# Hybrid trunk layer on one core: large loads on ScalarE's DMA queue, Gram matrices of the delta rule issued ahead of the substitution

## The chip, the cores and the metric

The kernel runs on one NeuronCore of a Trainium2 chip. TensorE (PE) multiplies matrices, VectorE (DVE), ScalarE (ACT) and GpSimd (POOL) work on tiles, and each of SyncE (SP), ScalarE and GpSimd can issue transfers. The metric is the time of one execution on the device, in microseconds, lower is better; several runs are made and their median is compared.

## The reference

One layer: RMSNorm of x with 16 learned meta tokens put in front (2048 + 16 tokens of 1024 channels), one projection to 8208 columns, two groups of heads on them, an output projection of 2048 channels added to x, and a final RMSNorm. Cut to what matters:

```python
h = rmsnorm(x, norm_g)
p = h @ w_in                                  # q k v | z | a b | sc_b sc_c sc_h sc_z
qkv = silu(causal_dwconv(qkv, dn_conv_w))     # width 4
q, k = l2norm(q) * 128 ** -0.5, l2norm(k)     # 8 heads x 128
g = -exp(A_log) * softplus(a + dt_bias); beta = sigmoid(b)
# gated delta rule in chunks, with decay = exp(g_i - g_j):
a_low = strict_lower(beta_i * (k k^T) * decay)
u, w = solve(I + a_low, [v * beta, k * beta * exp(g)])
for each chunk:                               # the scan over chunks
    v_new = u - w S
    o = (q exp(g)) S + ((q k^T) * decay) v_new
    S = S * exp(g_last) + (k exp(g_last - g))^T v_new
o_dn = rmsnorm(o, dn_out_g) * silu(z)
o_sc = sc_b * causal_dwconv(sc_c * sc_h, sc_conv_w) * silu(sc_z)
return rmsnorm(x + concat(o_dn, o_sc) @ w_out, final_g)
```

## The kernel before

All is float32; a large matmul is done as three float32r matmuls on parts hi and lo (hi x hi, lo x hi, hi x lo), so a weight tile is needed as `wh` and `wl`.

The first phase runs over two halves of 1024 tokens (the first with the meta tokens). A half has 64 jobs: 8 slots (one for each head and one eighth of the short convolution) of 8 column tiles of 128 (k, q, v, z and the four of the short convolution). A job (`run_group`, L745) runs three groups of tokens, each 24 matmuls into one of the PSUM tiles `mm`, which ScalarE or VectorE evacuates (`raw`, `acc`, `sc_c`, `zs`). `load_w` (L716) fetches a job's 512 KB of `w_in` into one of the two tiles `wr`; `split_w` (L722) makes `wh` on ScalarE and `wl` on VectorE in two halves, and gives the load of the job after the next right behind the second.

Beside the jobs run streams, Python generators that give work in small steps between a job's matmuls. `delta_front` (L971) does, for one half of one head at a time (a "half head", 16 in all; here "head 14" counts them from 0): the decays `E`, the Gram matrices k k^T and q k^T of two chunks of 128 tokens at a time (their operands' hi and lo parts in tile `nb`), the triangular matrices `M` and `P`; then the diagonal 32 x 32 blocks of `M` go by DRAM (`nbd`) into `nb`, where 31 rows of a substitution on VectorE (`substitution`, L942: a product `prod<-nb,XT` and a sum `XT<-prod` for each) give their inverses `XT`, which go to DRAM (`xtd`). `delta_back` loads these into `W`, transposes them (`X`) and merges them by matmuls (`ta<-X,E`) into the inverses of whole chunks; `delta_scan` runs the recurrence (`rec`, `vn`, `S`, `os`), `delta_out` norms and stores the outputs.

A small model of the engines (L30 to L100), written into the program, decides when a stream gives its next step; the order on each engine's queue is fixed when the program is built. A generator can also wait on a key in `done`, or on a tile in `held` (`hold`, L590). All engines' work goes through one recorder, so every row says L118: a tile's name tells what it is.

All transfers are issued by SP, in one queue: the weight loads, the small round trips by `nbd` and `xtd`, the decays, the gates and the stores `mixd` of the outputs. The second phase multiplies `mixd` by `w_out`; `load_mix` (L1425) brings the mixed channels of a tile of 128 tokens into `wr`.

Of the kernel before, what the change touches and what calls it, by code (L numbers as in the profile page):

```python
# [29 lines left out]
class Model:  # L30
    """Time of each engine and of each tile, as work is issued; it decides the order of issue only."""
# [32 lines left out]
    def after(self, *aps, slot=None, eng=None, lag=0.0, least=0.02):  # L64
        """Time until the tiles are written, the slot is free and the engine is through but for lag."""
# [96 lines left out]
class Recorded:  # L162
    """The engines of a core, with all that they are given entered into the model."""

    def __init__(self, nc, model):
        self.tensor = _Engine(nc.tensor, "PE", model)
        self.vector = _Engine(nc.vector, "DVE", model)
        self.scalar = _Engine(nc.scalar, "ACT", model)
        self.gpsimd = _Engine(nc.gpsimd, "POOL", model)
        self.sync = _Engine(nc.sync, "DMA", model)  # L170


@with_exitstack
def hybrid_trunk(
# [41 lines left out]
    # ---- order of emission: a stream of projections, cut into pieces, and streams of dependent  # L216
    # steps that are issued between the pieces. `model` follows the engines as they are given work;
    # a step yields the time until what its successor needs is there.
# [28 lines left out]
    def when_done(fn, ap, most=100.0):  # L247
        """Issue fn once ap has been written."""
        timed.append((clk() + min(after(ap), most), fn))
# [46 lines left out]
    def newton(dst, a, y, t):  # L296
        """dst = y (1.5 - 0.5 a y^2): one Newton step for a ** -0.5 from y."""
# [19 lines left out]
    # ---- constants of the first phase  # L317
# [12 lines left out]
    # eyep[32 q + block, m, i] = (i == 8 q + m)  # L330
    eyep = vt(pp, [128, 8, 32], "eyep")
# [10 lines left out]
    def constants():  # L342
# [29 lines left out]
        nc.gpsimd.memset(eyep, 0.0)  # L372
        for q in range(4):
            for m in range(8):
                nc.gpsimd.memset(eyep[32 * q : 32 * q + 32, m, 8 * q + m : 8 * q + m + 1], 1.0)
# [13 lines left out]
    def turn(hf, xt, k0, i, col, n, g):  # L389
        """Channels 4 k0 .. 4 k0 + 3 of a token tile into h^T."""  # L390
# [18 lines left out]
    def statistics(xt, n, jk):  # L409
        """mean square + eps and its approximate power -0.5."""  # L410
# [6 lines left out]
    def rootmean(xt, n):  # L417
        """(mean square + eps) ** -0.5 by ACT and GpSimd."""
# [14 lines left out]
    def prologue0():  # L433
        """h^T = (RMSNorm(x))^T of the first half as float32r parts hi + lo, [channel, k, token]
        by group."""
# [100 lines left out]
    def normalize(i):  # L536
        """RMSNorm of token tile i of the second half, to DRAM until the first half is through."""
        xt = vt(dp, [128, NC, 128], "kd").rearrange("p c i -> p (c i)")
        nc.sync.dma_start(xt, xs[HALF + 128 * i :][:128])
        yield after(xt)  # L540
        st = statistics(xt, 128, vt(dp, [128, 1840], "gw", dt=BF16))
# [48 lines left out]
    def hold(tag="ta", keep=False):  # L590
        """Wait until no step holds tag over several yields; or hold it."""
# [7 lines left out]
    def gates(hf):  # L599
        """Token-major gate values [128, head, chunk]; on half 0 chunk 8 holds the meta tokens."""  # L600
# [21 lines left out]
        gw = vt(dp, [128, 920], "gw")  # L622
# [24 lines left out]
        # e = exp(-|a|), exp(-|b|), exp(min(b, 0))  # L647
# [11 lines left out]
        # log1p(e) = 2 atanh(s), s = e / (2 + e) <= 1 / 3  # L659
# [34 lines left out]
        nc.sync.dma_start(ged[hf, :Wd], gT[:Wd])  # L694
        G[hf] = dict(beta=beta, gcum=gcum, neg=neg, nch=nch)
# [3 lines left out]
    # ---- projections  # L699
    class Job:  # L700
        def __init__(self, hf, col, init, consume, fin=None, skip=False):
# [8 lines left out]
            self.begun = False  # L710

# [3 lines left out]

    def load_w(j):  # L716
        if j < len(jobs):
            J = jobs[j]
            J.wr = vt(wp, [128, KT, 128], "wr")
            nc.sync.dma_start(J.wr, win[:, :, J.col : J.col + 128])  # L720

    def split_w(j, eng=None):  # L722
        if j >= len(jobs):
            return
        J = jobs[j]
        J.wh = vt(wp, [128, KT, 128], "wh", dt=F32R)
# [3 lines left out]
        if eng is not None:  # L730
            eng.tensor_tensor(out=J.wl, in0=J.wr, in1=J.wh, op=ALU.subtract)
            load_w(j + 2)
# [3 lines left out]
        def half(i):  # L736
            s_ = slice(4 * i, 4 * i + 4)
            nc.vector.tensor_tensor(out=J.wl[:, s_], in0=J.wr[:, s_], in1=J.wh[:, s_], op=ALU.subtract)
            if i == 1:
                load_w(j + 2)  # L740
# [35 lines left out]
    def conv_job(hf, s, col, t, pre, emit):  # L776
        """Projection, causal width-4 convolution and SiLU of channel tile t of q | k | v."""
# [43 lines left out]
    def slot_jobs(hf, s):  # L821
# [51 lines left out]
        # short convolution of channel tile s  # L873
# [67 lines left out]
    # ---- gated delta rule  # L941
    def substitution(nb, XT, prod):  # L942
        """Rows of (I + N)^-1 of unit lower triangular 32 x 32 blocks, a block and 8 columns per
        partition; nb[j, i] = N[i, j], XT[col, i], prod[col, i] = identity on entry."""
# [9 lines left out]
    def decay(hf, row0, n, E, gc):  # L954
        """E[j, c, i] = exp(g_i - g_j) for i >= j, else 0."""
# [14 lines left out]

    def delta_front():  # L971
        """Decays, the two triangular matrices, and the inverses of the diagonal blocks."""
        for i in range(2 * NH):
# [14 lines left out]
            )  # L988
            if hf == 0:
                Em = vt(dp, [NM, 1, NM], "mE")  # L990
# [20 lines left out]
            for c2 in range(4):  # L1011
                c0 = 2 * c2
                yield after(slot=(dp, "nb"))
                kp = vt(dp, [128, 2, 2, 2, 128], "nb", dt=F32R)
# [11 lines left out]
                for c in range(2):  # L1026
# [4 lines left out]
                    mmr(o_, lhsT=l_[:, :128], rhs=h_, start=False, stop=True)  # L1031
                yield after(pm, E)
# [27 lines left out]
            # inverses of the 32 x 32 diagonal blocks: partition 32 q + 8 b + c, columns 8 q .. 8 q + 7  # L1060
# [8 lines left out]
            if hf == 0:  # L1069
                yield from meta_inputs(hd, g_, d, Em)  # L1070
            yield after(nb)
# [12 lines left out]
            nc.gpsimd.tensor_copy(prod, eyep)  # L1084
# [20 lines left out]
            half[i] = dict(M=M, P=P, cd=cd, ir=ir, cj=cj)  # L1105
            done.add(("front", i))

    def delta_back():
        """The inverses of the whole chunks, and what the scan needs by token."""
        for i in range(2 * NH):  # L1110
# [11 lines left out]
            # q exp(g); token-major k, q norms, v  # L1122
# [514 lines left out]
```

## Time and profile before

| what | value |
| --- | --- |
| median of 3 runs | 2257.49 us (2250.55 to 2260.83) |
| span of the profiled execution | 2248.0 us, 9.5 below the median and 2.6 below the fastest run |
| TensorE busy | 2175.4 us (97%) |
| VectorE, ScalarE, GpSimd busy | 1456.6, 864.9, 153.3 us |

The busy share is an average over a start in which the pipeline fills, 16 slots of projections and a second phase of matmuls alone. The span less TensorE's time is what a change of order can take away; which wait ends last is read from the waits and from the timeline at each place. A wait is named by engine, the tile whose instruction waited, and what ended it; "issue" is a wait for which the profile shows no releaser.

### The profile page before, as it was taken

What the parts mean: (1) busy time and instruction counts of PE and PEld (TensorE: products, weight loads), DVE (VectorE), ACT (ScalarE), POOL (GpSimd) and SP (SyncE); (2) the same over time, 40 slices, a digit from 0 to 9 for tenths busy, and PEclk for the clock granted to TensorE, in tenths of its full rate; (3) what the DMA queues carried; (4) which work ended last, traced back from release to release, by engine and by line L of the source; (5) the groups of instructions that cost most, each with busy time, mean ns of one, the idle gap of its engine ahead of it and who ended that gap; (6) DMA issues with size and microseconds to landing.
All of it is one profiled execution on the core that took longest, in us unless ns stands there. A gap on an engine that the chain in (4) does not pass through costs nothing.

```text
span 2248.0 us, 38710 instructions
## 1 busy us (share of the span) xinstructions
PE 2175.4 (97%) x15024; PEld 2061.8 (92%) x15024; DVE 1456.6 (65%) x4031; ACT 864.9 (38%) x2080; POOL 153.3 (7%) x312
## 2 busy tenths in 40 slices
PE   6999999999999999999999999999998799999998
PEld 6999999999999998999999999999998798888886
DVE  4676867676767767776868677676766465544322
ACT  5534434444444333443434343525352324422111
POOL 4000100000000000101000000000000000000000
PEclk9999999999999999999999999999999899999999
DMA  6444345443535677524343544253546664645321
GB/s 140 75 81 70 84 68 91 67 93 67 92 67 104 82 83 60 134 43 80 52 83 57 78 52 83 48 88 43 88 49 60 53 94 139 222 164 189 119 94 57
DMA packets 257237, 196.46 MB, mean 87 GB/s; under 512 B 62085, under 2 KB 226446, under 8 KB 257054
## 3 DMA queue, kind: packets, MB, share of 16 engines
q1 hardware_dynamic: 257054, 194.00, 47.5%
q8 instruction: 118, 1.93, 0.4%
q14 instruction: 65, 0.53, 0.1%
HBM read 157.89 MB, written 36.06 MB: 86 GB/s over the span
## 4 chain that ended last, share of the span: by engine, by line
PE 87%; DMA 6%; DVE 4%; SPq 1%; ACT 1%; issue 1%; POOL 0%; POOLq 0%; DVEq 0%; ACTq 0%
PE mm L118 74%; PE ta L118 7%; PE rec L118 4%; PE o L118 2%; SPq L118 1%; DMA nb<-nbd 1%; DMA wr<-in_w_in_dram 1%; DMA kd<-in_x_dram 1%; DVE prod L118 1%; DMA xtd<-XT 1%; DMA W<-xtd 1%; ACT junk L118 1%; DVE acc L118 1%; DVE XT L118 1%; DMA nbd<-E 0%
## 5 line engine op out<-in xcount | busy, mean ns | idle before, releaser
L118 PE MATMUL mm<-hh,wh 128*128 128x384 f32 (+3 forms) x3328 | 1043.6, 335 | 6.4 <-ACT hh L118 5.3
L118 PE MATMUL mm<-hl,wh 128*128 128x384 f32 (+3 forms) x3328 | 1015.1, 326 | 0.0
L118 PEld LDWEIGHTS mm<-hh,wh 128*128 128x128 f32 x3328 | 626.8, 189 | 21.0 <-ACT hh L118 5.9
L118 PEld LDWEIGHTS mm<-hl,wh 128*128 128x128 f32 x3328 | 627.3, 189 | 9.7
L118 PE MATMUL mm<-hh,wl 128*128 128x384 f32 (+3 forms) x3200 | 622.6, 327 | 2.8 <-DVE wl L118 2.8
L118 PEld LDWEIGHTS mm<-hh,wl 128*128 128x128 f32 x3200 | 512.6, 189 | 9.9 <-DVE wl L118 3.2
L118 DVE TENSOR_TENSOR wl<-wr,wh 128x512 fp32r<-128x512 f32 x348 | 233.8, 691 | 98.8 <-ACT wh L118 67.0
L118 DVE SCALAR_TENSOR_TENSOR acc<-raw,pcol,acc 128x384 f32<-128x384 f32 (+2 forms) x432 | 245.5, 573 | 60.5 <-ACT acc L118 55.9
L118 ACT ACTIVATE wh<-wr 128x1024 fp32r<-128x1024 f32 x178 | 187.8, 1055 | 79.3 <-PE mm L118 44.5
L118 DVE SCALAR_TENSOR_TENSOR prod<-nb,XT 128x8 f32<-128x8 f32 (+30 forms) x496 | 192.8, 389 | 39.1 <-DMA nb<-nbd 34.0
L118 DVE TENSOR_REDUCE XT<-prod 128x8 f32<-128x16 f32 (+30 forms) x496 | 147.2, 297 | 17.0
L118 ACT ACTIVATE raw<-mm 128x272 f32<-128x272 f32 (+2 forms) x144 | 65.7, 456 | 214.1 <-PE mm L118 214.1
L118 ACT ACTIVATE vn<-rec,cj 128x128 f32<-128x128 f32 x128 | 46.9, 366 | 252.0 <-PE rec L118 246.7
L118 ACT ACTIVATE sc_c<-mm 128x384 f32<-128x384 f32 (+4 forms) x99 | 45.0, 456 | 161.8 <-PE mm L118 158.0
L118 PE MATMUL mm<-oh,wh 128*128 128x512 f32 x256 | 101.9, 398 | 0.0
L118 PE MATMUL mm<-ol,wh 128*128 128x512 f32 x256 | 100.3, 392 | 0.0
L118 DVE TENSOR_TENSOR y<-mm,y 128x512 f32<-128x512 f32 x23 | 15.9, 692 | 110.7 <-PE mm L118 110.7
L118 DVE SCALAR_TENSOR_TENSOR yy<-rec,neg,vr 128x128 f32<-128x128 f32 x128 | 44.4, 347 | 62.3 <-PE rec L118 61.8
L118 ACT ACTIVATE ojk<-y 128x512 bf16<-128x512 f32 x23 | 14.5, 631 | 182.6 <-DVE y L118 127.0
L118 ACT ACTIVATE acc<-mm,pcol 128x272 f32<-128x272 f32 (+2 forms) x144 | 78.2, 543 | 0.0
L118 DVE SCALAR_TENSOR_TENSOR S<-S,egl,rec 128x128 f32<-128x128 f32 x104 | 35.8, 344 | 59.2 <-PE rec L118 58.3
L118 POOL TENSOR_TENSOR opy<-mo,nhalf 128x4 f32<-128x4 f32 x32 | 35.3, 1102 | 544.0 <-DVE mo L118 507.3
(244 smaller groups left out, 2548.8 us busy)
## 6 DMA issues: line engine op xcount, KB each, us to landing
wr<-in_w_in_dram SPq DMA_DIRECT2D x128, 512.0 KB, 9.0
wr<-mixd SPq DMA_DIRECT2D x50, 512.0 KB, 4.5
E<-gtd SPq DMA_DIRECT2D x16, 512.0 KB, 4.1
qd<-ged SPq DMA_DIRECT2D x16, 512.0 KB, 8.4
nb<-nbd SPq DMA_DIRECT2D x64, 128.0 KB, 5.3
mixd<-zs SPq DMA_DIRECT2D x32, 256.0 KB, 3.2
out_dram<-y SPq DMA_DIRECT2D x16, 512.0 KB, 2.6
mixd<-sc_y SPq DMA_DIRECT2D x32, 192.0 KB, 2.4
```

The costliest lines, as they stand in the source:

```text
L118: r = real(*args, **kw)
```

## The change

Three things are changed; comments and docstrings go too.

1. A helper `bulk` issues a transfer on ScalarE's queue. The 128 weight loads use it, and the mix loads of the first eight tiles (32). The load of job j + 2 is no longer given right behind the second half of `wl` but when the model says that this is done; `split_w` gives it if it hasn't come. The model books 0.4 us of ScalarE for it.
2. `delta_front` ends with the Gram matrices. The blocks' way by `nbd` and `nb`, the substitution and the store to `xtd` become a stream of their own, `delta_inverse`, which waits for the Gram of its half head; `delta_front` meanwhile goes on to the next. The hi and lo parts of k and q move from tile `nb` to `gw`, which is guarded by `hold` against `gates` and `normalize`.
3. The identity for the substitution (`prod`) is made by a memset and four selects on GpSimd; before it was copied from a tile `eyep`.

```diff
+        self.bulk = _Engine(nc.scalar, "DMA", model)
...
+    def bulk(out_, in_):
+        nc.bulk.dma_start(out_, in_)
+        model.free["ACT"] = max(model.free["ACT"], clk()) + ISSUE
...
     def load_w(j):
-        if j < len(jobs):
+        if j < len(jobs) and jobs[j].wr is None:
             J = jobs[j]
             J.wr = vt(wp, [128, KT, 128], "wr")
-            nc.sync.dma_start(J.wr, win[:, :, J.col : J.col + 128])
+            bulk(J.wr, win[:, :, J.col : J.col + 128])
...
         J = jobs[j]
+        load_w(j)
...
             if i == 1:
-                load_w(j + 2)
+                when_done(lambda: load_w(j + 2), J.wl)
...
+                while i and ("meta", i - 1) not in done:
+                    yield 0.3
                 Em = vt(dp, [NM, 1, NM], "mE")
...
-                yield after(slot=(dp, "nb"))
-                kp = vt(dp, [128, 2, 2, 2, 128], "nb", dt=F32R)
+                yield after(slot=(dp, "gw"))
+                yield from hold("gw", True)
+                kp = vt(dp, [128, 2, 2, 2, 128], "gw", dt=F32R)
...
+                held.discard("gw")
...
-            # inverses of the 32 x 32 diagonal blocks: partition 32 q + 8 b + c, columns 8 q .. 8 q + 7
+            fronts[i] = (M, Em)
+            half[i] = dict(M=M, P=P, cd=cd, ir=ir, cj=cj)
+            done.add(("gram", i))
+
+    def delta_inverse():
+        for i in range(2 * NH):
+            hf, hd = divmod(i, NH)
+            while ("gram", i) not in done:
+                yield 0.3
+            d, g_ = slot[i], G[hf]
+            M, Em = fronts[i]
             nb = vt(dp, [128, 32, 32], "nb")
...
-            nc.gpsimd.tensor_copy(prod, eyep)
+            nc.gpsimd.memset(prod, 1.0)
+            for q in range(4):
+                nc.gpsimd.affine_select(
+                    out=prod[32 * q : 32 * q + 32],
...
         mr = vt(wp, [128, KT, 128], "wr")
-        nc.sync.dma_start(mr, mixd[u[0], :, KT * h : KT * h + KT])
+        (bulk if u[0] < NC else nc.sync.dma_start)(mr, mixd[u[0], :, KT * h : KT * h + KT])
```

The instructions of TensorE and VectorE stay the same in number. SP's transfers fall by 160 and ScalarE's rise by 160. Three places show the order.

On SP, around the inverse of head 14 (half head 6 of the second half), before, from the load of the blocks to the load of the inverses:

```order
L118 DMA nb<-nbd 32x1024 x4
L118 DMA qd<-ged 128x1024
L118 DMA mixd<-zs 128x4x128
L118 DMA wr<-in_w_in_dram 128x8x128 x4
L118 DMA mixd<-sc_y 128x2x128
L118 DMA mixd<-sc_y 128x3x128
L118 DMA xtd<-XT 32x8x32 x4
L118 DMA mixd<-sc_y 128x3x128
L118 DMA wr<-in_w_in_dram 128x8x128
L118 DMA W<-xtd 32x8x32 x4
```

The same place after:

```order
L118 DMA nb<-nbd 32x1024 x4
L118 DMA qd<-ged 128x1024
L118 DMA mixd<-zs 128x4x128
L118 DMA mixd<-sc_y 128x2x128
L118 DMA mixd<-sc_y 128x3x128
L118 DMA xtd<-XT 32x8x32 x4
L118 DMA mixd<-sc_y 128x3x128
L118 DMA W<-xtd 32x8x32 x4
```

The five weight loads that stood between `nb` and `W` are gone from SP's queue; the small transfers keep their order.

On ScalarE, at the end of the scan of head 13, before (`vn` and `os` belong to the scan, `raw` and `acc` evacuate a projection):

```order
L118 ACTIVATE wh<-wr 128x1024
L118 ACTIVATE vn<-rec,cj 128x128 x2
L118 ACTIVATE os<-o 128x512
L118 ACTIVATE junk,mo<-os 128x128 x4
L118 ACTIVATE wh<-wr 128x1024 x2
L118 ACTIVATE raw<-mm 128x256
L118 ACTIVATE acc<-mm,pcol 128x256
```

The same place after:

```order
L118 DMA wr<-in_w_in_dram 128x8x128
L118 ACTIVATE vn<-rec,cj 128x128
L118 ACTIVATE wh<-wr 128x1024
L118 ACTIVATE vn<-rec,cj 128x128
L118 ACTIVATE os<-o 128x512
L118 ACTIVATE junk,mo<-os 128x128 x4
L118 DMA wr<-in_w_in_dram 128x8x128
L118 ACTIVATE wh<-wr 128x1024
L118 ACTIVATE raw<-mm 128x256
L118 ACTIVATE acc<-mm,pcol 128x256
L118 DMA wr<-in_w_in_dram 128x8x128
```

Weight loads now stand among ScalarE's instructions, here one ahead of `vn`, one ahead of `wh` and one behind `acc`.

On VectorE, where the Gram of head 5 begins (`cd` copies its decays, `nb<-k,nb` and `nb<-q,nb` are the low parts of k and q, `P<-ta,E` takes the result), before, behind the last row of head 4's substitution:

```order
L118 COPY cd<-E 128x8
L118 TENSOR_TENSOR sc_u<-mm,sc_c 128x384
L118 TENSOR_TENSOR vr<-ta,ir 128x512
L118 TENSOR_TENSOR sc_y<-mm,sc_y 128x256
L118 TENSOR_SCALAR sc_y<-sc_u,pcol 128x384
L118 SCALAR_TENSOR_TENSOR sc_y<-sc_u,pcol,sc_y 128x384 x2
L118 TENSOR_TENSOR wl<-wr,wh 128x512
L118 TENSOR_TENSOR nb<-k,nb 128x2x128
L118 TENSOR_TENSOR nb<-q,nb 128x2x128
L118 STREAM_TRANSPOSE X<-W 32x8x32 x3
L118 TENSOR_TENSOR sc_y<-mm,sc_y 128x384
L118 TENSOR_TENSOR P<-ta,E 128x256
```

The same after, where these rows use the tile `gw`:

```order
L118 TENSOR_TENSOR wl<-wr,wh 128x512
L118 SCALAR_TENSOR_TENSOR prod<-nb,XT 128x8x25
L118 TENSOR_REDUCE XT<-prod 128x8
L118 TENSOR_TENSOR gw<-k,gw 128x2x128
L118 TENSOR_TENSOR gw<-q,gw 128x2x128
L118 SCALAR_TENSOR_TENSOR prod<-nb,XT 128x8x26
L118 TENSOR_REDUCE XT<-prod 128x8
L118 SCALAR_TENSOR_TENSOR prod<-nb,XT 128x8x27
L118 TENSOR_REDUCE XT<-prod 128x8
L118 TENSOR_TENSOR P<-ta,E 128x256
L118 TENSOR_TENSOR E<-ta,E 128x256
```

The low parts for head 5 now stand between rows 25 and 26 of head 4's substitution; the rows `prod<-nb,XT` go on behind them.

## Rows read from the trace of the kernel before

**Rows 1.** The page: busy time, share and instructions of each engine.

```profile
PE 2175.4 (97%) x15024; PEld 2061.8 (92%) x15024; DVE 1456.6 (65%) x4031; ACT 864.9 (38%) x2080; POOL 153.3 (7%) x312
```

**Rows 2.** Windows; columns: stretch, width, PE, PEld, DVE, ACT, POOL, PEclk, DMA share, GB/s.

```profile
0.00:50.00 50.00, 30.95 (x184) 28.48 (x185) 23.89 (x39) 26.84 (x48) 26.90 (x105) 1.00 0.68 157
...
500.00:600.00 100.00, 99.95 (x758) 97.09 (x757) 70.03 (x225) 41.02 (x109) 7.32 (x15) 1.00 0.41 75
```

**Rows 3.** Waits of PE, whole run: total us, times, longest us.

```profile
PE ta L118 <- issue: 15.0, 3, 13.6
...
PE rec L118 <- DVE os L118: 10.5, 5, 6.4
...
PE rec L118 <- DVE S L118: 7.4, 3, 3.5
...
PE ta L118 <- DVE X L118: 3.8, 2, 3.2
```

**Rows 4.** Timeline of PE: start, us, what, and in brackets the idle before.

```profile
1705.95 1.12 PE L118 MATMUL rec<-ident,os 128*128 128x128 f32 x4 [6.39 <-DVE os L118]
...
1773.24 1.48 PE L118 MATMUL ta<-X,E 32*32 32x32 f32 x32 [13.61 <-issue]
```

**Rows 5.** Timeline of DVE at the ends of its waits.

```profile
802.43 0.17 DVE L118 SCALAR_TENSOR_TENSOR prod<-nb,XT 128x8 f32<-128x8 f32 x1 [3.98 <-DMA nb<-nbd]
...
1702.65 0.17 DVE L118 SCALAR_TENSOR_TENSOR prod<-nb,XT 128x8 f32<-128x8 f32 x1 [8.72 <-DMA nb<-nbd]
...
1772.71 1.37 DVE L118 STREAM_TRANSPOSE X<-W 32x256 f32<-32x256 f32 x3 [15.91 <-DMA W<-xtd]
...
1821.60 0.17 DVE L118 SCALAR_TENSOR_TENSOR prod<-nb,XT 128x8 f32<-128x8 f32 x1 [5.20 <-DMA nb<-nbd]
```

**Rows 6.** Waits of DVE, whole run: total us, times, longest us.

```profile
DVE prod L118 <- DMA nb<-nbd: 34.0, 10, 8.7
...
DVE X L118 <- DMA W<-xtd: 20.9, 3, 15.9
```

**Rows 7.** Timeline of SP, the issue of transfers, 1755 to 1775.

```profile
1756.41 0.39 SPq L118 DMA_DIRECT2D wr<-in_w_in_dram  x1
...
1759.56 4.91 SPq L118 DMA_DIRECT2D W<-xtd  x4
```

**Rows 8.** DMA issues, 400 to 700: count, KB each, median us to landing.

```profile
wr<-in_w_in_dram SPq DMA_DIRECT2D x21, 512.0 KB, 8.7
...
xtd<-XT SPq DMA_DIRECT2D x12, 32.0 KB, 4.4
...
W<-xtd SPq DMA_DIRECT2D x12, 32.0 KB, 1.9
```

**Rows 9.** DMA issues, 1660 to 1840.

```profile
wr<-in_w_in_dram SPq DMA_DIRECT2D x10, 512.0 KB, 14.0
...
xtd<-XT SPq DMA_DIRECT2D x4, 32.0 KB, 9.5
...
W<-xtd SPq DMA_DIRECT2D x4, 32.0 KB, 13.0
```

**Rows 10.** Windows around TensorE's stops (columns as in group 2).

```profile
880.00:890.00 10.00, 10.00 (x116) 9.18 (x116) 4.82 (x15) 3.23 (x6) 0.00 (x0) 0.80 0.57 27
...
1690.00:1712.00 22.00, 15.61 (x90) 15.29 (x89) 9.79 (x33) 3.20 (x11) 1.31 (x3) 0.84 0.57 75
...
1752.00:1772.00 20.00, 7.63 (x49) 7.14 (x46) 0.77 (x2) 7.68 (x22) 0.10 (x1) 0.81 0.93 84
...
1772.00:1785.00 13.00, 11.61 (x153) 10.56 (x154) 7.53 (x19) 4.97 (x11) 0.00 (x0) 0.76 0.21 33
```

**Rows 11.** The page: costliest groups of instructions, the low part of a weight tile.

```profile
L118 DVE TENSOR_TENSOR wl<-wr,wh 128x512 fp32r<-128x512 f32 x348 | 233.8, 691 | 98.8 <-ACT wh L118 67.0
```

**Rows 12.** Groups of POOL by shape: count, busy us, mean ns, idle before.

```profile
L118 POOL COPY prod<-eyep 128x256 f32<-128x256 f32 x16 | 6.6, 411 | 0.0
...
L118 POOL TENSOR_SCALAR_AFFINE_SELECT mE<-mE 16x16 f32<-16x16 f32 x8 | 3.0, 369 | 1.1 <-DVE mE L118 1.1
```

More of the change, by code (lines that the diff above doesn't have):

```diff
@@ L329, in hybrid_trunk @@
     triu = vt(pp, [128, 128], "triu")
-    eyep = vt(pp, [128, 8, 32], "eyep")
     W = vt(pp, [128, NC, 128], "W")
@@ L371, in constants @@
         nc.gpsimd.memset(X[0:64], 0.0)
[L372 to L375, printed above, removed]
         nc.scalar.activation(negA, negA, AF.Exp)
@@ L540, in normalize @@
         yield after(xt)
+        yield from hold("gw")
         st = statistics(xt, 128, vt(dp, [128, 1840], "gw", dt=BF16))
@@ L621, in gates @@
         pt = ptile(pta, "ta", [128, 512])
-        gw = vt(dp, [128, 920], "gw")
+        yield from hold("gw", True)
+        gw = vt(dp, [128, 1024], "gw")
         ab2 = gw[:, 0:288].rearrange("p (c m) -> p c m", m=32)
@@ L710, in __init__ @@
             self.begun = False
+            self.wr = None
     jobs = []
@@ L739, in half @@
             if i == 1:
-                load_w(j + 2)
+                when_done(lambda: load_w(j + 2), J.wl)
         later(lambda: half(0))
@@ L969, in hybrid_trunk @@
     half = {}
+    fronts = {}
     def delta_front():
@@ L988, in delta_front @@
             )
+            Em = None
             if hf == 0:
+                while i and ("meta", i - 1) not in done:
+                    yield 0.3
                 Em = vt(dp, [NM, 1, NM], "mE")
@@ L1012, in delta_front @@
                 c0 = 2 * c2
-                yield after(slot=(dp, "nb"))
-                kp = vt(dp, [128, 2, 2, 2, 128], "nb", dt=F32R)
+                yield after(slot=(dp, "gw"))
+                yield from hold("gw", True)
+                kp = vt(dp, [128, 2, 2, 2, 128], "gw", dt=F32R)
                 kh, kl = kp[:, 0], kp[:, 1]
@@ L1031, in delta_front @@
                     mmr(o_, lhsT=l_[:, :128], rhs=h_, start=False, stop=True)
+                held.discard("gw")
                 yield after(pm, E)
@@ L1070, in delta_front @@
                 yield from meta_inputs(hd, g_, d, Em)
+            done.add(("meta", i))
             yield after(nb)
@@ L1083, in delta_front @@
             prod = vt(dp, [128, 8, 32], "prod")
-            nc.gpsimd.tensor_copy(prod, eyep)
+            nc.gpsimd.memset(prod, 1.0)
+            for q in range(4):
+                nc.gpsimd.affine_select(
+                    out=prod[32 * q : 32 * q + 32],
+                    in_=prod[32 * q : 32 * q + 32],
+                    pattern=[[-1, 8], [1, 32]],
+                    compare_op=ALU.is_equal,
+                    fill=0.0,
+                    base=-8 * q,
+                    channel_multiplier=0,
+                )
             rows = [substitution(nb, XT, prod)]
@@ L1104, in delta_front @@
                 )
-            half[i] = dict(M=M, P=P, cd=cd, ir=ir, cj=cj)
             done.add(("front", i))
@@ L1377, in delta_out @@
             yield 0.3
+    ISSUE = 0.4
     STEP = 1.0
@@ L1493, in hybrid_trunk @@
     start(delta_front())
+    start(delta_inverse())
     start(delta_back())
```

## The prediction

> **What bounds the kernel now.** I read the engine lines first: TensorE is busy 2175.4 of 2248.0 us, VectorE 65%, ScalarE 38%, GpSimd 7% [rows 1]. So a change can only gain in TensorE's 72.6 us of idle time and in what TensorE loses at a low clock; no matmul is added or removed here. The table of windows says where that is not: 500 to 600 us has 99.95 us of work in 100 at full clock, while the first 50 us have 30.95, that is 19.0 us of idle before anything is in the buffers [rows 2]. The waits of TensorE name the rest [rows 3]: 15.0 us of `ta` behind "issue", 10.5 `rec` behind `os`, 7.4 `rec` behind `S`, 3.8 `ta` behind `X`.
>
> Each large wait is then followed one engine back. TensorE stops 6.39 us before 1705.95, and 13.61 us before 1773.24 [rows 4]. VectorE at these places stood before its own first product of the substitution (8.72 us, `nb<-nbd`, until 1702.65) and before the transposes of `W` (15.91 us, `W<-xtd`, until 1772.71). It did so too ahead of the three `S` waits, each time for `nb`: 3.98 us at 802.43 in the first, 5.20 at 1821.60 in the last [rows 5]. Over the whole run VectorE waits 34.0 us for `nb` in 10 places and 20.9 us for `W` in 3 [rows 6]. Those are loads of 128 KB. The reader is to see in SP's timeline why they are late: at 1756.41 SP issues a weight tile of 512 KB, at 1759.56 the four `W` loads, which come to use 13 us later [rows 7]. Between 400 and 700 us a `W` load lands 1.9 us after its issue and a weight tile 8.7; between 1660 and 1840 these are 13.0 and 14.0, and `xtd` 9.5 [rows 8, 9]. `W` takes as long as the weight load ahead of it: one queue serves them in their order.
>
> **What the change does to this.** Part (a): 128 weight tiles and 32 mix tiles leave SP's queue for ScalarE's. In the first pair of orders SP had five weight loads between the `nb` loads and the `W` loads of this head; now it has none. So the 13.0 us should fall towards 1.9. What goes with it: 13.6 (the long one of the "issue" waits), 6.4 of `os`, 7.4 of `S` and 3.8 of `X`, together 31.2 us.
>
> With the idle time a second cost goes. Around each of these stops the granted clock is below 1, and half clock is the 1.2 GHz level. The time lost is the window by what the mean clock lacks, by TensorE's busy share there [rows 10]: 880 to 890: 10 x 0.20 x 1.00 = 2.0; 1690 to 1712: 22 x 0.16 x 0.71 = 2.5; 1752 to 1772: 20 x 0.19 x 0.38 = 1.4; 1772 to 1785: 13 x 0.24 x 0.89 = 2.8. That is 8.7; with the shorter dips, which I didn't add up, I take 10 us. The least is 4.8, from 880 to 890 and 1772 to 1785 alone, where TensorE was busy; in the others the low clock may have fallen in the idle part. Together 41 us are to be had.
>
> Not all of it goes. Weight tiles of the last slot land in 14.0 us and not 8.7, and the DMA share was 0.93 at 84 GB/s in 1752 to 1772: the 16 engines were busy with slow transfers, and `W` on its own queue still shares them. If it got half of these 84 GB/s, its 4 x 32 KB would take 3.1 us, with the 1.9 of an undisturbed one 5; `xtd` the same, so the round trip is 10 us, against 9.5 + 13.0 = 22.5 before and 4.4 + 1.9 = 6.3 in the middle of the first half [rows 8, 9]. The order gives the round trip about 10 to 14 us of TensorE work before the transposes come (my count of the instructions between, 75 to 105 rows at the 99.95 / 758 = 0.13 us of rows 2). So it is met at the edge. I keep a quarter of the 41, 10 us; the bounds are 0 (round trip 6.3) and 41 (nothing is won, below).
>
> The Trainium skill, "DMA: Bandwidth & Descriptors", section "Issuing engines are not separate DMA queues", speaks against the change: transfers that different engines initiate run on the same 16 DMA engines, and a second initiating engine only saves the sequencer its issue time. By that sentence alone the sum would be about 0. The section "Queues, rings and completion order" of the same page gives SP and ScalarE a ring each on every engine, served in turn packet by packet; by that, `W` passes the load ahead of it. The 1.9 against 13.0 [rows 8, 9] shows only that order in one queue costs 11 us; no run of before has loads in two queues, so the first rule is kept as a rival.
>
> Part (a) has a price on ScalarE. A weight load takes 0.39 us of issue [rows 7], and ScalarE must stop at it until the second half of `wl` has been made (0.69 us of VectorE [rows 11]), because that tile's buffer is being refilled. Queued behind it are the evacuations of PSUM and the `vn` of the scan, for which TensorE waits. In the second pair of orders a load stands right ahead of `vn` and of `wh`. In the whole order 17 of the 128 stand right ahead of a `vn`, 55 ahead of an evacuation (`raw`, `sc_c`, `zs`). An evacuation has the other PSUM buffers' matmuls as cover; `vn` lies on the scan's chain, which has projections beside it. Bounds: 0, and 17 x (0.39 + 0.69) = 18. I take half of 17 x 0.39 = 6.6: 3 us. The mix loads of the second phase cost nothing: ScalarE is idle for most of that time; if not, 32 x 0.39 = 12, at the 18's side of the range.
>
> Part (b): the Gram matrices run ahead. The third pair of orders shows it: before, decay and Gram of head 5 come after the last row of head 4's substitution, now between its rows. No instruction is added, the hi and lo tile only changes its name from `nb` to `gw`, which frees `nb` sooner. TensorE is full there (the 99.95), so what becomes ready earlier waits in the queue. I cost it at 0. If its cover goes, it adds VectorE work between rows: two subtractions per pair of chunks, already counted in the 65%. From below: it could take the remaining 10 us away, as the substitution starts sooner.
>
> Part (c): `prod` by a memset and four selects on GpSimd in the place of one copy. The copy takes 0.411 and a 16x16 select 0.369 [rows 12]; with a memset counted like the copy that is 16 x 4 x 0.369 = 24 us more of GpSimd. VectorE's first copy waits for it, 1.5 us more per head. That lies behind the `nb` load, VectorE has a third of its time idle, and TensorE has projections to do: 0, with 24 as upper bound. At the start the third weight load now stands in ScalarE's queue ahead of its evacuations: 0, bounds 5 either way, a quarter of the 19.0 [rows 2].
>
> **The sum.** 2248.0 - 41 + 10 + 3 = 2220. The profiled execution is 9.5 us below the median of the three runs (2257.49; 2.6 below the fastest), so the median is 2229.5, in whole 2229. Own range: from 2211, where all of the 41 and 5 of the start are gained and nothing is paid, to 2246, where 23 of the 41 stay and 7 are paid.
>
> **Rivals.** (A) More: the round trip has its 6.3 us, the start gains its 5: 2248 - 41 - 5 + 9.5 = 2211. For it: the Gram is ahead, and `nb` comes free earlier. Against it: the slow loads of the last slot. Chance 0.12.
>
> (B) The 16 engines are the limit, not the queue: `W` and `nb` take as long beside a load as behind it. For it: share 0.93 at 84 GB/s [rows 10]. Against it: the share is 0.41 in 500 to 600 [rows 2], so most heads meet engines with room. What is left are the `S` waits, mostly away from the slow loads: 2257.5 - 7.4 + 3 = 2253. This is also what comes if the stops only move, for instance to the weight tiles: at 14.0 us each and eight jobs a slot the loads need 112 us, and with the idle gone TensorE needs little more. Chance 0.16.
>
> (C) Slower: ScalarE is held by the loads. Place: the 72 loads ahead of `vn` and the evacuations; price: 72 x (0.39 + 0.69) = 78 us if nothing covers them, since ScalarE stands at `wl` and everything that TensorE waits for is behind. It decides over the sign once (41 - 10) / 78 = 40% of it reach TensorE. At three quarters: 2226.5 + 58 = 2285; at half 2265. For it: VectorE's own stops (15.91) would now stop ScalarE too. Against it: ScalarE has 62% idle, and the order puts the load behind the `wl` by a little. Chance 0.12 of more than 0.5% slower.
>
> That the change doesn't do what it says: the orders show it does.
>
> **Chances.** 0.5% (11.3 us) is about what a measurement of this kernel can tell from no change: 2246.2 and 2268.8 are its ends. My forecast 0.60 and (A) 0.12 are faster: 0.72. (B) is the same: 0.16. (C) is slower: 0.12. The range, 2209 to 2257, holds (A) with 2 us for idle time that I didn't count, the forecast, and (B) up to the median of before; it leaves out (C).
>
> **What would show it.** Right: VectorE's 34.0 for `nb` and 20.9 for `W` fall below 20 together; `W` lands in 2 to 6 us between 1660 and 1840; TensorE's stops of 13.61 and 6.39 are gone and its clock there is 1. (B): the landing stays near 13. (C): new TensorE waits for ScalarE (`vn`, `mm` evacuations), with ScalarE idle ahead of a load for `wl`. Wrong altogether if TensorE's busy time grows without a lower clock.

## The result: slower, 2288.4 us

The changed kernel takes 2288.39 us (median of 4 runs, 2287.56 to 2289.44), the kernel before 2255.09 (4 runs beside it); the ratio is 1.0142, interval 1.0122 to 1.0162. 2229 was predicted, with a range up to 2257. The profiled execution spans 2285.6 us, 37.6 more than before.

The page's busy line, and its rows of the two hardware queues (packets, MB, share of 16 engines; q10 carries ScalarE's transfers, q1 SP's):

```profile
PE 2194.1 (96%) x15024; PEld 2071.0 (91%) x15024; DVE 1467.2 (64%) x4031; ACT 864.2 (38%) x2080; POOL 189.1 (8%) x343
...
q10 hardware_dynamic: 137728, 83.90, 30.8%
q1 hardware_dynamic: 119326, 110.10, 15.9%
```

Against [rows 1] TensorE is busy 18.7 us longer with the same 15024 instructions, and idle 91.5 us where it was 72.6. So half of the loss is waiting, and most of the other half is a lower clock: the mean granted clock is 0.984, before 0.991, which makes 2175.4 us of work 15.5 us longer. The windows show where, with the columns of [rows 2]:

```profile
0.00:50.00 50.00, 23.22 (x146) 21.10 (x147) 24.15 (x32) 22.71 (x41) 23.91 (x68) 1.00 0.65 157
500.00:600.00 100.00, 97.48 (x729) 94.15 (x727) 70.92 (x205) 38.09 (x102) 8.76 (x17) 1.00 0.39 82
205.00:225.00 20.00, 16.08 (x83) 14.01 (x82) 12.48 (x27) 7.36 (x29) 0.00 (x0) 0.78 0.74 140
268.00:284.00 16.00, 10.34 (x47) 8.45 (x46) 15.17 (x45) 4.90 (x12) 0.00 (x0) 0.69 0.33 58
1690.00:1712.00 22.00, 22.00 (x157) 22.00 (x156) 15.34 (x50) 8.97 (x22) 0.00 (x0) 1.00 0.43 31
1795.00:1815.00 20.00, 10.58 (x119) 9.57 (x120) 7.57 (x22) 2.47 (x6) 3.98 (x8) 0.54 0.43 50
```

The stretch 1690 to 1712, with the stop of 6.39 us before [rows 4, 10], is now full and at clock 1. But 205 to 225 and 268 to 284 have new dips to 0.78 and 0.69, 1795 to 1815 has 10.58 us of work at 0.54 where 1752 to 1772 was [rows 10], and 500 to 600 is no longer full. TensorE's largest waits (total, times, longest) put names to them:

```profile
PE ta L118 <- DVE vT L118: 17.3, 1, 17.3
PE rec L118 <- ACT vn L118: 10.1, 9, 2.1
PE ta L118 <- DVE X L118: 9.8, 1, 9.8
PE ta L118 <- issue: 8.6, 4, 3.9
PE ta L118 <- DVE gw L118: 5.7, 3, 2.7
```

The waits for `os` and `S` [rows 3] fell from 10.5 and 7.4 to 4.1 and 5.4. New are those for `vn` and `gw`, and 10 us more at the start (`vT`, 17.3 where it was 6.8); one wait for `X` is still 9.8 us long. VectorE's waits for transfers, as in [rows 6]:

```profile
DVE X L118 <- DMA W<-xtd: 19.6, 5, 10.8
...
DVE vT L118 <- DMA sc_u<-in_norm_g_dram: 16.5, 1, 16.5
...
DVE prod L118 <- DMA nb<-nbd: 5.0, 3, 2.6
```

`nb` fell from 34.0 to 5.0, `W` only from 20.9 to 19.6. The issues of 400 to 700, then of 1660 to 1840, against [rows 8, 9]:

```profile
wr<-in_w_in_dram ACTq DMA_DIRECT2D x21, 512.0 KB, 8.7
...
xtd<-XT SPq DMA_DIRECT2D x12, 32.0 KB, 1.6
W<-xtd SPq DMA_DIRECT2D x12, 32.0 KB, 2.4
...
wr<-in_w_in_dram ACTq DMA_DIRECT2D x11, 512.0 KB, 13.8
...
xtd<-XT SPq DMA_DIRECT2D x8, 32.0 KB, 2.2
W<-xtd SPq DMA_DIRECT2D x8, 32.0 KB, 8.5
```

The weight loads land as before, `xtd` sooner, and the `W` loads of the last slot in 8.5 us, where 2 to 6 were the sign that the forecast was right.

To place the loss I lined up the traces by the first matmul of a job (job 64 opens the second half, the last column is a place in the second phase). Times are start in the kernel before, then microseconds later than it:

| kernel | job 8 | job 24 | job 64 | job 112 | job 124 | second phase |
| --- | --- | --- | --- | --- | --- | --- |
| before, start | 135.7 | 360.8 | 939.6 | 1618.2 | 1811.8 | 2150.9 |
| changed | 6.0 | 24.9 | 39.5 | 36.9 | 29.2 | 37.9 |
| part (a) alone (e1_queue) | 6.0 | 6.3 | 29.6 | 26.6 | 24.8 | 65.7 |
| parts (b), (c) alone (e2_gram) | -0.3 | 18.3 | 44.2 | 42.9 | 36.2 | 37.7 |
| the same, Gram ahead in the second half only (e16_half2) | -0.7 | 3.2 | 44.6 | 52.7 | 52.9 | 53.7 |

The changed kernel loses 6 us at the start, 33 in the rest of the first half, wins 10 back in the second, and loses 9 at the end. A job can also start late because other work was given ahead of it (the changed kernel is 37.5 us late at job 20), so single columns are rough. The runs of the last three rows are told below.

### The profile page after: what moved, and what is told of

Read it like the earlier page. It is cut to its first block, busy times and chain, and to the rows that moved or that the text cites. A ratio compares the mean times of both kernels' runs of the same rounds, so it can differ in the third digit from the quotient of the medians.

```text
span 2285.6 us, 38685 instructions
## 1 busy us (share of the span) xinstructions
PE 2194.1 (96%) x15024; PEld 2071.0 (91%) x15024; DVE 1467.2 (64%) x4031; ACT 864.2 (38%) x2080; POOL 189.1 (8%) x343
## 4 chain that ended last, share of the span: by engine, by line
PE 85%; DMA 6%; DVE 5%; ACT 3%; issue 1%; SPq 0%; POOL 0%; ACTq 0%; POOLq 0%; DVEq 0%
PE mm L118 71%; PE ta L118 7%; PE rec L118 4%; PE o L118 2%; DMA wr<-mixd 1%; DMA kd<-in_x_dram 1%; DMA Q<-in_norm_g_dram 1%; DVE prod L118 1%; ACT junk L118 1%; DMA W<-xtd 1%; DMA qd<-in_x_dram 1%; DVE XT L118 1%; DVE acc L118 1%; DVE wl L118 1%; DMA xtd<-XT 1%
## 5 line engine op out<-in xcount | busy, mean ns | idle before, releaser
L118 ACT ACTIVATE wh<-wr 128x1024 fp32r<-128x1024 f32 x178 | 187.9, 1056 | 97.6 <-DMA wr<-mixd 53.7
L118 ACT ACTIVATE raw<-mm 128x272 f32<-128x272 f32 (+2 forms) x144 | 65.7, 456 | 225.4 <-PE mm L118 224.9
L118 POOL TENSOR_TENSOR kpy<-ssk,nhalf 128x8 f32<-128x8 f32 x16 | 28.7, 1791 | 537.5 <-DVE ssk L118 471.4
```

The source lines that it names most:

```text
L118: r = real(*args, **kw)
```

## The experiments

Each was run in 5 rounds beside the kernel before. The medians:

| run | what | median us | ratio, interval |
| --- | --- | --- | --- |
| e1_queue | part (a) alone | 2305.9 | 1.0231 (1.0208 to 1.0253) |
| e2_gram | (b) and (c) alone | 2286.0 | 1.0138 (1.0119 to 1.0158) |
| e3_first | changed, first two weight loads on SP | 2287.2 | 1.0145 (1.0123 to 1.0166) |
| e4_mix | changed, mix loads on SP | 2276.7 | 1.0097 (1.0080 to 1.0115) |
| e5_gram2 | changed, Gram ahead in the second half only | 2320.6 | 1.0295 (1.0265 to 1.0325) |
| e6_cols | changed, the last slot's jobs load the first slot's columns | 2264.5 | 1.0036 (1.0023 to 1.0049) |
| e7_late | (a)'s time of giving, SP's queue | 2261.3 | 1.0033 (1.0021 to 1.0045) |
| e9_cols_before | before, the same | 2222.4 | 0.9852 (0.9833 to 0.9871) |
| e10_swap | before, slow column tiles shared out between two slots | 2240.1 | 0.9936 (0.9923 to 0.9949) |
| e11_rest | (a) without mix and first two loads | 2286.0 | 1.0141 (1.0122 to 1.0159) |
| e12_pool | e11's weight loads issued by GpSimd | 2274.3 | 1.0090 (1.0069 to 1.0110) |
| e15_prod | (c) alone | 2251.2 | 0.9986 (0.9978 to 0.9994) |
| e16_half2 | (b), (c), ahead in the second half only | 2306.1 | 1.0220 (1.0204 to 1.0237) |
| e17_half2_swap | the same with e10's exchange | 2297.2 | 1.0177 (1.0161 to 1.0193) |
| e18_swap_prod | before, e10's exchange and (c) | 2243.9 | 0.9949 (0.9934 to 0.9964) |
| e19_delay0 | before, first half's substitutions 5 us later | 2284.1 | 1.0123 (1.0102 to 1.0143) |
| e20_delay1 | before, second half's 5 us later | 2230.1 | 0.9890 (0.9870 to 0.9910) |
| e21_both | e10 and e20 | 2225.2 | 0.9866 (0.9849 to 0.9883) |

**The two parts apart.** e1_queue is the kernel before with the `bulk` helper, `load_w` and `load_mix` of the diff; e2_gram takes them out of the changed kernel:

```diff
-        nc.bulk.dma_start(out_, in_)
-        model.free["ACT"] = max(model.free["ACT"], clk()) + ISSUE
+        nc.sync.dma_start(out_, in_)
...
-                when_done(lambda: load_w(j + 2), J.wl)
+                load_w(j + 2)
```

> The kernel before with part (a) alone: weight loads and the first 32 mix loads on ScalarE's queue, given when wl is done; Gram matrices and substitution in one stream as before, prod copied as before. Theory 1 (part (b) puts the first head's chain late in the program's order and the start loses to two queues; the move of the loads itself gains): the start pays 6 to 8 us as in the changed kernel, the stops of 13.6, 6.4 and 7.4 mostly go, so 2230 to 2245 us, faster than before by 10 to 25. VectorE's wait for nb falls from 34.0 to under 10. Rival (ScalarE is held by the loads it issues, so vn, os and the evacuations come late): as slow as the changed kernel, 2270 to 2290.

> The changed kernel with all loads back on SP and given right behind wl: parts (b) and (c) alone. Theory 1: the 25 to 30 us lost in the first half stay, and the stops behind SP's queue come back, so 2280 to 2300 us. Rival (ScalarE is held by the loads): the loss goes, about the time before, 2250 to 2260.

Theory 1 fell for part (a): the move of the loads, for which I had forecast the whole gain, costs 52 us by itself. The rival fell as well: (b) and (c) lose 32 without it, as theory 1 had it for them. Neither part gains, and they don't add (52 + 32 against 33).

**Start and mix loads.**

```diff
-            bulk(J.wr, win[:, :, J.col : J.col + 128])
+            (bulk if j >= 2 else nc.sync.dma_start)(J.wr, win[:, :, J.col : J.col + 128])   # e3_first
...
-        (bulk if u[0] < NC else nc.sync.dma_start)(mr, mixd[u[0], :, KT * h : KT * h + KT])
+        nc.sync.dma_start(mr, mixd[u[0], :, KT * h : KT * h + KT])                        # e4_mix
```

> The changed kernel with the first two weight loads on SP, in their old place behind the first token tiles. Theory 1: the first transposes come 10 us sooner again and 6 to 8 us of it last: 2280 to 2283 us. Rival: the start is made up by the first jobs and the time stays at 2288.

> The changed kernel with the mix loads on SP. Theory 1: ScalarE no longer stands 53.7 us for its own mix loads; the waits for vn at 1901 and 1910 (3.9 us) and the low clock behind them go, so 4 to 8 us less, 2280 to 2284. Rival: the end is set by the last head's chain, which was late already: 2288, with the waits only put elsewhere.

The start hardly matters: 1.2 us, within the intervals (at job 8 it was 4 us), although in the changed kernel the broadcast of the norm's gain, issued 0.45 us behind the first weight load on the other queue, took 15.1 us, before 4.6:

```profile
sc_u<-in_norm_g_dram SPq DMA_DIRECT2D x1, 512.0 KB, 15.1
```

The mix loads cost 11.7 us, more than expected. The trace has the gain where the changed kernel lost its last 9 us: the second phase is 27.2 us late instead of 37.9. ScalarE's wait for its own loads, in the changed kernel and then in e4_mix (total, times, longest):

```profile
ACT wh L118 <- DMA wr<-mixd: 53.7, 21, 3.9
```

```profile
ACT wh L118 <- DMA wr<-mixd: 13.0, 4, 4.8
```

**What the queue changes.** e7_late gives the weight loads when part (a) does, but on SP; e11_rest is part (a) without the two items above; e12_pool issues e11's loads from GpSimd (`self.bulk = _Engine(nc.gpsimd, "DMA", model)`, no time booked on ScalarE).

> The kernel before with the weight loads still in SP's queue, but given when the model says that wl is done (part (a) without the other queue). Theory 2: the queue hardly matters, so this loses much of what part (a) alone lost (2306): 2275 to 2300. Rival (the other queue is what costs): about the time before, 2250 to 2262.

> Part (a) alone, with the mix loads and the first two weight loads left on SP: 126 weight loads on ScalarE's queue. Theory 3 (a weight load in a second queue is no longer held back by the small transfers that stand ahead of it in one queue; it starts first and they land behind it; besides, ScalarE is held up to 5 us at a load): 12 to 20 us less than part (a) alone, 2286 to 2294, so some 30 us above the same loads in SP's queue (2261). Rival (start and mix loads are all of the loss): 2255 to 2265.

> As the run before in this list, but the 126 weight loads are issued by GpSimd, which is idle 93% of the time and evacuates nothing. It parts the two halves of theory 3: if a load that overtakes the small transfers is what costs, 2280 to 2295, as with ScalarE; if ScalarE's hold at a load is, 2255 to 2265.

The same loads given at the same time cost 2261.3 in SP's queue, 2274.3 from GpSimd and 2286.0 from ScalarE. My expectation of e7_late, that the queue hardly matters, fell; that of e11_rest held. e12_pool (2267.6 to 2283.8) lies between its two cases: GpSimd in SyncE's place costs 13 us, ScalarE in GpSimd's 12. With the 7 us of e7_late and the 20 between e1_queue and e11_rest (mix loads and the first two weight loads) these are part (a)'s 52. The split is not clean: GpSimd's loads go by another kind of queue (`software_dynamic` on the page, 18144 packets where ScalarE's took 131040), each issue takes GpSimd 0.9 us, and e11_rest alone books time for the issue in the program's model.

Where the 13 us arise, the traces show at the last head. In one queue a small transfer that waits for its data holds back the weight load behind it: in e7_late the load starts behind the four `nb` loads. In e12_pool it starts ahead of them. SyncE's issues and VectorE of e7_late, then GpSimd, SyncE and VectorE of e12_pool:

```profile
1827.25 1.71 SPq L118 DMA_DIRECT2D nb<-nbd  x4
...
1829.52 0.45 SPq L118 DMA_DIRECT2D wr<-in_w_in_dram  x1
...
1831.83 0.17 DVE L118 SCALAR_TENSOR_TENSOR prod<-nb,XT 128x8 f32<-128x8 f32 x1 [5.57 <-DMA nb<-nbd]
...
1837.62 0.92 POOL L118 DMA_DIRECT2D wr<-in_w_in_dram  x1 [5.08 <-ACT vn L118]
...
1840.40 8.26 SPq L118 DMA_DIRECT2D nb<-nbd  x4
...
1855.28 0.17 DVE L118 SCALAR_TENSOR_TENSOR prod<-nb,XT 128x8 f32<-128x8 f32 x1 [17.41 <-DMA nb<-nbd]
```

VectorE waits 11.8 us longer there. Part (a) alone has the same at this place. Timeline of e1_queue, ACTq and SPq (issues) and VectorE:

```profile
1841.83 0.37 ACTq L118 DMA_DIRECT2D wr<-in_w_in_dram  x1
...
1842.42 9.58 SPq L118 DMA_DIRECT2D nb<-nbd  x4
...
1858.24 0.17 DVE L118 SCALAR_TENSOR_TENSOR prod<-nb,XT 128x8 f32<-128x8 f32 x1 [15.43 <-DMA nb<-nbd]
```

At 1841.83 the weight load starts 0.6 us ahead of the small ones; `nb` lands at 1858.1, and VectorE stands 15.43 us. ScalarE's own part is a hold at a load; e11_rest's timeline of ScalarE:

```profile
1770.45 1.15 ACT L118 ACTIVATE kd<-ta,cd 128x128 f32<-128x128 f32 x4 [0.75 <-PE ta L118]
1776.37 0.37 ACTq L118 DMA_DIRECT2D wr<-in_w_in_dram  x1
1776.79 0.28 ACT L118 ACTIVATE junk<-ta 128x128 bf16<-128x128 f32 x1 [5.20 <-DMA wr<-in_w_in_dram]
```

`junk<-ta` reads no weights: ScalarE could not go past the load, 5.20 us. The load itself stood until the weight load before it, issued at 1762.42, had landed (1776.27); `wl`, the wait that I had priced, had been over since 1769.76. The view of waits puts four more (two `vn`, `sc_c`, `zs`) down to weight loads, but in three of them the load had gone out 3.9 to 4.4 us before the wait ended, so they show no hold. What the holds cost in all is not counted; the 12 us are the difference of two runs.

**The slow loads.** In the last slot of each half the columns are the last eighth of each block. e6_cols (changed kernel) and e9_cols_before load the first slot's columns again in its eight jobs; they leave out the last eighth of the projection:

```diff
+            col = J.col - 896 * (J.col % 1024 // 16 in (56, 57))
-            nc.sync.dma_start(J.wr, win[:, :, J.col : J.col + 128])
+            nc.sync.dma_start(J.wr, win[:, :, col : col + 128])
```

> The changed kernel, but the eight jobs of the last slot load slot 0's columns of w_in, so the last eighth of the columns isn't used. Theory 2 with the slow loads a matter of their address: all weight loads land in 9 us, the small transfers behind them 5 us sooner, the wait of 9.8 us for X and those near 910 go: 2265 to 2278 us. Rival (the loads of the last slot are slow for what runs beside them): they still land in 14 us, time as the changed kernel.

> The kernel before, but the eight jobs of the last slot load slot 0's columns of w_in, so the last eighth of the columns isn't used. Theory 2: the stops of 13.6, 6.4, 3.5 and 3.8 us, all beside loads of the last slot, shrink by a half or more and the low clock behind them goes: 2225 to 2240 us. Rival (slow for what runs beside them): 2255.

The theory held in both, and both times came out just below their ranges: 24 us less in the changed kernel, 32 in the one before, in which the weight loads of that time now land in 9.6 us instead of 14.0 [rows 9]:

```profile
wr<-in_w_in_dram SPq DMA_DIRECT2D x11, 512.0 KB, 9.6
```

So the columns make these loads slow, and the stops of [rows 4] came from them: behind the start no wait of TensorE in e9_cols_before is over 4.0 us. e10_swap moves four of the eight to the first slot and leaves nothing out:

```diff
+        cs = (7, 1, 2, 3, 4, 5, 6, 0)[s]
-        base = 4 * D + 16 + s * 128
+        base = 4 * D + 16 + cs * 128      # and cs for s in ucar, stap and mixd's channel tile
```

> The kernel before, with the short convolution's channel tiles 0 and 7 exchanged between the first and the last slot, so that four of the eight slow weight loads (columns of the last eighth) come in each half's first slot and four stay in the last; the whole computation is done. Theory 2 (slow loads are a matter of the columns, and they cost by the small transfers that land behind them): the load ahead of the W of 13.6 us is now a fast one, half of the gain of the run with all eight replaced (32 us): 2235 to 2245. Rival: the slow loads of the first slot of the second half stop the last head of the first half as much: 2250 to 2260.

It held: 14 us less, 0.64% faster than before. Its trace shows the slow loads move with the columns: near the start of the second half four loads take 13.6 to 19.0 us where the kernel before has 8.4 to 9.4, in the last slot four take 9.0 to 10.8 where it has 13.7 to 15.8.

**Part (c).** e15_prod is the kernel before with the memset and the selects of the diff.

> The kernel before with part (c) alone, prod by a memset and four selects on GpSimd. It costs VectorE 1.5 us at the head of each substitution, behind a wait for nb that is longer: no change, 2252 to 2260. If GpSimd's work is on the chain: up to 24 us more.

No cost; 0.14% less is too little to build on, and e18_swap_prod, with both edits, didn't show it again.

> The kernel before with part (c) and the exchange of tiles 0 and 7 in the first and last slot. If the 3 us of part (c) and the 14 of the exchange add: 2235 to 2239. If part (c)'s were a shift of one stop: 2240.

2243.9 against 2240.1: the 3 us don't add.

**Part (b).** The changed kernel's and e2's TensorE rows show stretches without a projection. In e2_gram, near 729 us:

```profile
728.28 0.60 PE L118 MATMUL mm<-hh,wl 128*128 128x384 f32 x2
...
730.19 0.49 PE L118 MATMUL rec<-vn,kd 128*128 128x128 f32 x2 [1.09 <-ACT vn L118]
...
733.30 0.49 PE L118 MATMUL rec<-yy,W 128*128 128x128 f32 x2 [1.47 <-DVE yy L118]
...
738.54 0.80 PE L118 MATMUL rec<-vn,kd 128*128 128x128 f32 x2 [0.52 <-ACT vn L118]
...
739.41 0.57 PE L118 MATMUL mm<-hh,wh 128*128 128x272 f32 x1
```

From 728.7 to 739.4 only scan steps run, each waiting for the last; a projection (`mm`) comes first at 739.41. The three longest of these in e2 are 8.8, 12.9 and 10.9 us from one projection's matmul to the next, at 206, 263 and 729; 7.6 and 8.0 follow at 883 and 937. e5_gram2 and e16_half2 hold the Gram matrices back in the first half:

```diff
+            while hf == 0 and i and ("front", i - 1) not in done:
+                yield 0.3
             E = vt(dp, [128, NC, 128], "E", bufs=2)
```

> The changed kernel, with the Gram matrices ahead of the substitution in the second half of the tokens only; in the first half each waits for the substitution of the head before, as in the kernel before. Theory 2 (two causes: in the first half the Gram matrices push the first heads' chain back, so that the program must give scan steps with no projections between them; and a small transfer lands only when the weight load under way does, whichever queue issued it): the drains at 213 and 270 us and their low clock go, 15 to 25 us less, 2263 to 2273 us. Rival (the order is not what costs, ScalarE held by its loads is): 2288, the same losses in other places.

> Parts (b) and (c) alone (all loads on SP), with the Gram matrices ahead of the substitution in the second half of the tokens only. Theory 4 (the 32 us of parts (b) and (c) alone are the first half's order: three times the program gives 9 to 13 us of one head's chain with no projection between, because that head's chain is late behind the next one's Gram): 2245 to 2260, and of the three stretches without projections at 207, 264 and 729 us at most one stays. Rival (the second stream and the guarded tile cost by themselves): 2275 to 2290.

> The run before in this list with the short convolution's tiles 0 and 7 exchanged between the first and the last slot. If both gains add: 8 to 15 us below it, 2232 to 2250. If the Gram matrices of the second half, given earlier, already avoid the long stop at 1773: the same as it.

The ranges of all three were missed: the three stretches went (7.1, 7.6 and 10.1 us at 792, 850 and 915 are left in e16_half2), and the time rose by 32 and 20 us. The exchange of tiles took 9 us off e16_half2, as expected, from a high level. The lined-up starts say more: at job 24 e16_half2 is 3 us late and not 18, so the Gram matrices ahead did cost that; at job 64 it is as late as e2_gram (45 and 44), and what it loses more comes in the second half, which the edit does not touch itself. So the three stretches are not what the 32 us hang on. e19_delay0 and e20_delay1 test, in the kernel before, whether the chain of a head (substitution, merge, scan) has room beside a full TensorE:

```diff
             yield after(nb)
+            if hf == 0:          # e20_delay1: hf == 1
+                yield 5.0
```

> The kernel before, with every substitution of the first half given 5 us later in the program (a pause of the stream, no other edit). Theory 5 (in the first half a head's chain is as long as a slot, so its lengthening is paid): 8 pauses of 5 us, less a slack of a few us in all: 2275 to 2295, with stretches of scan steps without projections. Rival (TensorE is full, the chain has room): 2250 to 2262.

> The same pause of 5 us in the second half's substitutions only. Theory 5: the second half's chain is shorter than a slot (no meta tokens, no normalisation of further tokens beside it), so the pauses cost less than half of those in the first half: 2252 to 2272. Rival (both halves alike): the same loss as in the first half.

e19_delay0 held: 8 pauses of 5 us cost 28. So in the first half a longer chain is paid for, although TensorE is full; that the chain is as long as a slot fits this and is not measured. e20_delay1 went the other way: 26 us faster than before. With the pause VectorE reaches the substitution later, when `nb` has mostly arrived, and its waits for `nb` and `W` fall from 54.9 to 23.2 us (against [rows 6]):

```profile
DVE prod L118 <- DMA nb<-nbd: 11.8, 6, 3.8
...
DVE X L118 <- DMA W<-xtd: 11.4, 6, 5.3
```

> The kernel before with the pause of 5 us ahead of the second half's substitutions (2230 alone) and the exchange of the short convolution's tiles 0 and 7 between the first and last slot (2240 alone). If they take away different stops: 2214 to 2222. If both take away the same one at 1773 us, which is 13.6 us and its low clock: 2226 to 2234.

2225.2, between the two cases: the gains of 26 and 14 add up to 30 only. It is the fastest version that leaves nothing out, 1.3% faster than the kernel before beside it and, by the medians, 2.8% than the changed one.

## Why the prediction was wrong

**The step that failed first: "the 13.0 us should fall towards 1.9", and behind it "if it got half of these 84 GB/s" 5 us.** The stop at 1773 is the test. In the changed kernel it lies at 1804 (ScalarE's and SP's issue, VectorE, TensorE):

```profile
1787.86 0.37 ACTq L118 DMA_DIRECT2D wr<-in_w_in_dram  x1
...
1788.57 6.94 SPq L118 DMA_DIRECT2D W<-xtd  x4
...
1803.75 1.37 DVE L118 STREAM_TRANSPOSE X<-W 32x256 f32<-32x256 f32 x3 [10.78 <-DMA W<-xtd]
...
1804.33 1.44 PE L118 MATMUL ta<-X,E 32*32 32x32 f32 x32 [9.84 <-DVE X L118]
```

ScalarE issues a weight load at 1787.86, SP the `W` loads at 1788.57, on the other queue. The weight load lands at 1803.51, the first `W` load at 1803.72, after 15.15 us; TensorE stops 9.84 us. Two queues gave `W` no share: it landed when the load ahead of it in time had landed, as in one queue, where it took 13.0 behind a load [rows 9]. The packets say the same. Of those that started from 1789 to 1800 every one is of ScalarE's queue (packets, MB, share of 16 engines):

```profile
q10 hardware_dynamic: 900, 0.46, 92.8%
```

Over all small transfers issued while a weight load was under way (`nbd`, `nb`, `xtd`, `W`, beside fast and slow loads apart), the median landing is 0.2 to 1.8 us behind that load's in every group, in the kernel before and in part (a) alone. Of those whose landing the trace has, none of 52 landed ahead of the load with one queue; with two, 3 of 34 did, by 0.2 to 7.1 us, each issued within 0.5 us of the load. The Trainium skill, "DMA: Bandwidth & Descriptors", section "Issuing engines are not separate DMA queues", says that DMAs of all issuing engines run on the same 16 engines and that a second issuing engine saves only the time of the issue. The trace agrees as to the shared engines: `W` came 15.15 us after its issue. The turn-taking between queues, packet by packet, that the Trainium skill states on the same page in "Queues, rings and completion order" doesn't show in the 900 packets.

So rival (B)'s mechanism was right, and its price too low: a queue of its own also lets the load go ahead of the small transfers. With GpSimd's queue that is 13 us (e12_pool against e7_late), 11.8 of it seen at the last head, and no term of my sum had it.

**"Part (b) ... I cost it at 0", since TensorE is full.** It is the second failed step: 32 us with all loads on SP. A full TensorE doesn't say that a chain beside it has room. In the changed kernel TensorE's projections (`mm`) stop near 270 us and begin again at 282.56; between, scan steps wait up to 2.1 us for the one before, and the granted clock of 268 to 284 is 0.69:

```profile
269.43 0.60 PE L118 MATMUL mm<-hh,wl 128*128 128x384 f32 x2
...
272.37 0.49 PE L118 MATMUL rec<-vn,kd 128*128 128x128 f32 x2 [2.13 <-ACT vn L118]
...
273.87 0.60 PE L118 MATMUL rec<-S,k 128*128 128x128 f32 x2 [0.79 <-DVE S L118]
...
279.13 0.79 PE L118 MATMUL rec<-S,k 128*128 128x128 f32 x2 [1.23 <-DVE S L118]
...
282.56 0.57 PE L118 MATMUL mm<-hh,wh 128*128 128x272 f32 x1
```

e19_delay0 shows that lengthening the first half's chain is paid for; that parts (b) and (c) lengthen it is what the lined-up starts say (18 us by job 24, 44 by job 64). Holding the Gram matrices back took the first away (3 us by job 24) and not the second (45 by job 64); what costs between these jobs is open.

**ScalarE's price, 3 us, bounds 0 and 18.** Measured 12 for ScalarE in GpSimd's place (e11_rest against e12_pool), inside the bounds, and 12 for the mix loads (e4_mix), which I had at 0 with 12 as its end. That both are inside is in part luck: I priced the issue and 0.69 us of `wl`, while the hold of 5.20 us waited for the landing of the load before, and with the mix loads went ScalarE's wait for their data. Rival (C) had this place, with 39 us at half and 58 at three quarters of its price; the latter gives 2285, near the measured time, but by luck, as it had neither the overtaking nor part (b).

**What was right.** VectorE's waits for `nb` and `W` fell together to 24.6 from 54.9, though not below 20, and the stop of 6.39 us and its clock loss went. But not by the queue: in part (a) alone the `nb` waits grew, from 34.0 to 51.8 us. Parts (b) and (c) alone brought `nb` and `W` down to 22.5 and 9.3. That the substitution there starts later after its load is likely and not traced; e20_delay1, which starts it later, has that gain without the rest. The last slot's loads at 14 us, of which I kept a quarter of the loss, were the larger thing: 32 us in e9_cols_before. The start (0, bounds 5) was 6 us by job 8 and 1 at the end; part (c) was 0, as costed.

**Open.** Why the parts don't add, what parts (b) and (c) lose between jobs 24 and 64, and why the Gram matrices ahead in one half alone cost more than in both.

## What to carry to other kernels

When small transfers wait behind large ones, a second queue need not cure it; here it gave them almost no share. Make the large ones shorter or move them, or give the consumer of the small one later in its engine's order, so that nothing stands behind its wait. An order in one queue may be what holds a large transfer back until the small ones have gone. Before a chain beside a full engine is called free, delay it by a known amount and see whether the time moves.

## What the runs showed of the hardware

Loads of 512 KB of a matrix with 32,832-byte rows, 512 bytes of each, land in 9 us for most columns and in 14 us for the last 128 of each block of 1024 (medians of the last slot 13.8 and 14.0 in the two kernels); with the first columns in their place, 9.6; moved to another slot, they are slow there (e10_swap). An engine that issues transfers can be held at one for 5 us with its own work waiting behind, here until the load before had landed (e11_rest). A 32 KB load takes 1.9 us alone and 15.15 beside a slow 512 KB load that another queue issued 0.71 us earlier; for 11 us of these only the load's packets started. Of 34 small transfers issued while such a load was under way in another queue, three landed before it, each issued within 0.5 us of it (e1_queue).
